# Tokens 256 to 511 first in the input projection of a decoder block

## The chip, the core and the metric

The program runs on one core of a Trainium2 chip. Its engines are TensorE (PE in the profile, with its weight loads shown apart as PEld), VectorE (DVE), ScalarE (ACT), GpSimd (POOL) and SyncE (SP, which issues the DMAs here). The metric is the device time of one execution in microseconds, as the median of several runs. All arithmetic is in 32-bit floats, and a product is formed from operands that are split into a high and a low part.

## The reference

The reference is one layer of a hybrid decoder: 16 meta tokens are put ahead of 1024 tokens of width 1024, each token is normalized, and a wide projection feeds three mixers (windowed attention with sinks and a relative bias, forgetting attention, and a gated linear recurrence). Their outputs are gated, summed and projected; a SwiGLU block and a last normalization follow. What the change touches is the beginning:

```python
h = jnp.concatenate([meta, x], axis=1)             # 16 + 1024 tokens
u = rms_norm(h, norm_mix[l])
proj = u @ w_in[l]
qa, ka, va, qf, kf, vf, fl, xc, yc, gates = jnp.split(proj, split_points, axis=-1)
```

and the table of relative biases, `rel_table[t5_bucket(dist)]`, which windowed attention adds to its scores much later.

## The kernel before

Tokens are taken in nine tiles: tile 0 holds the 16 meta tokens, tiles 1 to 8 hold 128 tokens each. A tile goes through three steps. `load_x` issues its DMA (512 KB for a full tile). `normed` (line 292) squares it on ScalarE with a sum along the row (line 297), takes the root (line 298), inverts it on VectorE (line 299) and multiplies the tile, in two halves, by that factor and the gains `gbc` (line 301). `to_feature_major` (line 198) transposes eight blocks of 128 by 128 on TensorE (line 204) into two PSUM banks, and `split` (line 115) writes the high part from each bank with ScalarE (line 118) and the low part with VectorE (line 119), into the token columns of `uh` and `ul`.

The projection is computed feature by feature. One block of 128 features needs the weights of that block, 512 KB, loaded by `load_w` and split into a high and a low tile; with `lo_on_pool=True` the low one is formed on GpSimd (line 138), otherwise on VectorE. `proj_chunk` multiplies one such block with a chunk of token columns: 8 blocks of the inner dimension, with three matmuls each (high by high, high by low, low by high; line 150), so 24 matmuls in one PSUM bank, which a sink then copies out on ScalarE. `FULL` cuts the 1040 token columns into chunks of 272, 256 and 512; `REAL` cuts the 1024 real tokens into two of 512. The columns 272 to 527 are tiles 3 and 4.

This first stage projects four blocks, `XC`, `XC+1` (inputs of the recurrence) and `YC`, `YC+1` (its gates), and forms the table of biases: a small matmul `pb` (line 321), an addition (line 322), a store to `bts` in DRAM, a load of 1.5 MB back into all partitions as `bb`, and a store of that as `bss`. Before the change the order written is: tiles 0, 1 and 2; the small loads and `pb`; the weights of `XC`; tiles 3 and 4; chunk 272 and chunk 256 of both `XC` blocks; the weights of `YC`; the other tiles among the remaining chunks.

A planner orders each engine's instructions at compile time. It takes the written order as priority, but lets an instruction go ahead of earlier ones when by its own estimate its inputs are there sooner. Engines then run their queues strictly in that order. `keep_in_program_order(i)` holds `i` behind the instruction written just before it on its engine. `issue_after(i)` holds all that a block writes for the engine of `i` behind `i`, without waiting for its end. Pools give tiles a number of buffers (4 for `xt`, the raw tokens; 2 for `wr`, the raw weights; 2 PSUM banks for transposes): a DMA into a buffer waits until the last reader of the tile before is done, and all DMAs are issued from one queue, SP's, in its order. The pool `r0` of this stage is closed after it, and the tiles of the next stages lie on the same addresses; a tile waits for the readers of those tiles that lay there.

After this stage come the blocks `XC+2` and `YC+2`, and then `values`, which loads four pieces of `w_v`, splits them into `vh` and `vl` and uses them as moving operands.

## Time and profile before

| | |
|---|---|
| median of 3 runs | 1662.85 us (1662.39 to 1664.62) |
| the profiled execution | 1662.29 us, of which the profile's span is 1660.5 us |
| TensorE matmuls busy | 1630.2 us, 98% of the span |
| VectorE, ScalarE, GpSimd busy | 999.4 us, 760.7 us, 433.1 us |
| mean granted clock of TensorE | 0.996 |

The span is cut into 40 slices of 41.5 us on the profile's page. There TensorE is at 9 tenths or more in all slices but three: the first (7), one near 1060 us (8) and the last (8). The profile's chain of work that ended last is 87% TensorE. All times of the rows below count from the start of the span.

### The profile page before, as it was taken

To read this page: it belongs to the slowest core of one execution; us is meant where nothing else is said; L and a number is where in the kernel's file an instruction comes from. 1 tells how busy PE (TensorE), PEld (TensorE's weight loads), DVE (VectorE), ACT (ScalarE), POOL (GpSimd) and SP (SyncE) were. 2 spreads that over 40 slices of the span, in tenths; PEclk is the share of its full clock that TensorE was granted. 3 is DMA by queue.
4 is the path that set the end of the run, shared out by engine and by line. 5 is a ranking of instruction groups with operands and counts; after the bars stand their busy time and mean duration, and the time that the engine had idled before them with its cause. 6 is when DMAs were issued, how large, how long until landed. Compare 5 with 4: busy or idle time off the path is not lost.

```text
span 1660.5 us, 22597 instructions
## 1 busy us (share of the span) xinstructions
PE 1630.2 (98%) x8159; PEld 1375.1 (83%) x8159; DVE 999.4 (60%) x1799; ACT 760.7 (46%) x1397; POOL 433.1 (26%) x341
## 2 busy tenths in 40 slices
PE   7999999999999999999999999899999999999998
PEld 6898978888888888888887888688888888888886
DVE  6565556555566666641348437977666676567544
ACT  6456466555555555542336434333333333345342
POOL 2111001001122221110225001776666566300000
PEclk9999999999999999999999999899999999999999
DMA  7132352223324142339737221464444443598642
GB/s 255 63 108 93 122 153 79 88 89 121 108 76 129 59 122 79 107 114 320 244 127 235 102 77 70 158 222 169 165 147 146 146 161 131 197 356 278 195 128 101
DMA packets 110879, 242.47 MB, mean 146 GB/s; under 512 B 11944, under 2 KB 23544, under 8 KB 110512
## 3 DMA queue, kind: packets, MB, share of 16 engines
q1 hardware_dynamic: 110768, 241.04, 42.7%
q8 instruction: 64, 1.05, 0.3%
q14 instruction: 47, 0.39, 0.1%
HBM read 163.45 MB, written 72.21 MB: 142 GB/s over the span
## 4 chain that ended last, share of the span: by engine, by line
PE 87%; DVE 4%; issue 4%; ACT 2%; POOL 1%; DMA 1%; SPq 0%; DVEq 0%; POOLq 0%; ACTq 0%
PE mm_w L150 26%; PE mm_s L150 13%; PE tr_s L150 7%; PE mm_br L150 6%; PE mm_wo L150 5%; PE mm_x L1086 4%; PE tr_y L1086 4%; PE sc_y L1086 4%; PE ob L547 3%; PE sc_s L150 3%; PE tr L558 3%; PE mm_v L150 2%; PE ob_x L1086 1%; PE mm_g L150 1%; PE mm_u L150 1%
## 5 line engine op out<-in xcount | busy, mean ns | idle before, releaser
L150 PE MATMUL mm_w<-uh,wh 128*128 128x512 f32 (+2 forms) x744 | 292.6, 393 | 0.0
L150 PE MATMUL mm_w<-uh,wl 128*128 128x512 f32 (+2 forms) x744 | 280.5, 377 | 0.0
L150 PE MATMUL mm_w<-ul,wh 128*128 128x512 f32 (+2 forms) x744 | 279.9, 376 | 0.0
L150 PEld LDWEIGHTS mm_w<-uh,wl 128*128 128x128 f32 x744 | 140.0, 188 | 25.7
L150 PEld LDWEIGHTS mm_w<-uh,wh 128*128 128x128 f32 x744 | 140.4, 189 | 12.7
L150 PEld LDWEIGHTS mm_w<-ul,wh 128*128 128x128 f32 x744 | 140.7, 189 | 11.7
L119 DVE TENSOR_TENSOR ab<-raw,ab 128x1024 fp32r<-128x1024 f32 x77 | 93.0, 1224 | 71.6 <-ACT ab L118 69.6
L118 ACT ACTIVATE ab<-raw 128x1024 fp32r<-128x1024 f32 x77 | 80.9, 1059 | 94.7 <-PE ob_x L1086 23.4
L150 PE MATMUL mm_s<-pt,ar 128*128 128x512 f32 x480 | 117.4, 394 | 3.7 <-ACT c L952 3.7
L118 ACT ACTIVATE wh<-wr 128x1024 fp32r<-128x1024 f32 (+1 forms) x85 | 72.7, 856 | 103.2 <-PE mm_w L150 50.6
L150 PE MATMUL mm_br<-o,wh 128*128 128x512 f32 x384 | 118.3, 389 | 0.0
L119 DVE TENSOR_TENSOR pl<-tr,ph 128x384 fp32r<-128x384 f32 (+2 forms) x160 | 87.4, 555 | 47.0 <-ACT ph L118 43.1
L150 PEld LDWEIGHTS mm_s<-pt,ar 128*128 128x128 f32 x480 | 91.5, 191 | 23.6 <-ACT c L952 4.5
L118 ACT ACTIVATE ph<-tr 128x384 fp32r<-128x384 f32 (+2 forms) x160 | 76.8, 485 | 53.6 <-PE tr L558 51.5
L119 DVE TENSOR_TENSOR wl<-wr,wh 128x1024 fp32r<-128x1024 f32 x45 | 55.6, 1235 | 72.2 <-ACT wh L118 71.9
L648 POOL TENSOR_SCALAR s<-s,sm 128x144 f32<-128x144 f32 (+3 forms) x64 | 48.6, 761 | 172.1 <-DVE sm L647 144.2
L150 PEld LDWEIGHTS mm_br<-o,wh 128*128 128x128 f32 x384 | 72.1, 188 | 14.9
L558 PE MATMUL tr<-ident,s 128*128 128x128 f32 x480 | 79.6, 274 | 1.2 <-POOL s L596 0.6
L150 PE MATMUL mm_wo<-woh,hl 128*128 128x512 f32 x256 | 79.1, 390 | 0.0
L150 PE MATMUL mm_br<-o,wl 128*128 128x512 f32 x192 | 75.3, 392 | 1.5 <-DVE wl L119 1.4
L558 PEld LDWEIGHTS tr<-ident,s 128*128 128x128 f32 x480 | 59.1, 140 | 18.3 <-DVE pl L119 3.4
L1086 PE MATMUL mm_x<-ab 128*128 128x512 f32 x297 | 72.7, 389 | 0.0
(252 smaller groups left out, 3687.9 us busy)
## 6 DMA issues: line engine op xcount, KB each, us to landing
wr<-w_in_dram SPq DMA_DIRECT2D x45, 512.0 KB, 3.7
wr<-w_fi_dram SPq DMA_DIRECT2D x44, 512.0 KB, 3.8
raw<-asp SPq DMA_DIRECT2D x77, 256.0 KB, 3.2
asp<-a SPq DMA_DIRECT2D x66, 256.0 KB, 2.5
gz<-z SPq DMA_DIRECT2D x48, 256.0 KB, 2.1
o<-osp SPq DMA_DIRECT2D x24, 512.0 KB, 6.1
sg<-gz SPq DMA_DIRECT2D x48, 256.0 KB, 3.2
fo<-w_fo_dram SPq DMA_DIRECT2D x22, 512.0 KB, 5.1
```

Source lines behind the costliest of these rows:

```text
L118: act.activation(hi, src, AF.Copy)
L119: i = dve.tensor_tensor(lo, src, f32(hi), ALU.subtract)
L150: pe.matmul(ps, a, b, start=first and i == 0, stop=i == n - 1, skip_group_check=not first)
L547: pe.matmul(ob[:, q0:q0 + b - a], vt[:, c], x[:, a:b], start=count == 0, stop=count == n_mm - 1, skip_group_check=True)
L558: pe.transpose(tb[:, col:col + P], src, ident)
L648: pool.tensor_scalar(s[:, :nk], s[:, :nk], den, 1.0, ALU.mult, ALU.mult)
L1086: pe.matmul(banks[x], a[:, 0, q], b[:, 1], start=first and j == 0 and c == 0, stop=j == NJ - 1 and c % 3 == 2, skip_group_check=True)
```

## The change

The stage is written in a new order:

- `split` returns its two instructions, and `to_feature_major` returns those of its second half.
- 16 transposes of the identity are put at the head of TensorE's work; their results are not used. After the transposes of tile 3, and again after those of tile 4, come 8 more whose results are not used.
- Tiles 3 and 4 are loaded first, the gains between them, then the weights of the two `XC` blocks. The split of each block of weights is held on ScalarE behind the second high part of tile 3 or 4, and its low part is formed on VectorE. The weights of `YC` are split on VectorE too.
- The chunk of 256 columns of both `XC` blocks is projected first; tiles 1, 2 and 0, in this order, are loaded after the weights of `XC`, and their work on ScalarE is held behind the second high part of tile 4.
- The 512 columns of `YC` that were one chunk are two of 256: columns 272 to 527 come second, columns 16 to 271 after the chunk of 272 of both `XC` blocks.
- `pb`, its addition and `nsink` are held behind all the chunks, and so the transfers `bts`, `bb` and `bss` come after them as well.

```diff
     def split(hi, lo, src, scale=None, pin=False):
 
         if scale is None:
-            act.activation(hi, src, AF.Copy)
+            a = act.activation(hi, src, AF.Copy)
             i = dve.tensor_tensor(lo, src, f32(hi), ALU.subtract)
...
+        return a.ins, i.ins
...
-            split(uh[:, ks, off:off + n], ul[:, ks, off:off + n], src)
+            last = split(uh[:, ks, off:off + n], ul[:, ks, off:off + n], src)
+        return last
...
-        xts = [load_x(t) for t in range(2)]
+        def busy(x, n, k):
+
+            for i in range(k):
+                pe.transpose(spare[:, :n], x[:n, i * P:(i + 1) * P], ident[:n, :n])
+
+        spare = o_bank("_spare")
+        for _ in range(16):
+            busy(ident, P, 1)
+
+        xts = {3: load_x(3)}
         dma(gbc, gains[0:1].partition_broadcast(P))
-        xts.append(load_x(2))
-        n0, n1 = normed(0, xts[0]), normed(1, xts[1])
-        to_feature_major(*n1)
-        n2 = normed(2, xts[2])
-        to_feature_major(*n0)
-        to_feature_major(*n2)
+        xts[4] = load_x(4)
+        raws = []
+        for m in range(2):
+            raws.append(wp.tile([P, D], F32, tag="wr", name=nm("wr")))
+            dma(raws[m], w_in[XC + m])
+        sinks = [x_sinks(ra, m) for m in range(2)]
+        wx = []
+        ns = [normed(t, xts[t]) for t in (3, 4)]
+        for n, raw in zip(ns, raws):
+
+            seen = to_feature_major(*n)[0]
+            with tc.issue_after(seen):
+                hi, lo = (r0.tile([P, D], F32R, name=nm("wx")) for _ in range(2))
+                split(hi, lo, raw)
+                wx.append((hi, lo))
+            busy(n[0], P, 8)
+        xts = {t: load_x(t) for t in (1, 2, 0)}
+        wy = [load_w(w_in[YC + m], D) for m in range(2)]
+        for m in range(2):
+            run(proj_chunk(XC + m, wx[m], FULL[1], sinks[m][0]))
+        with tc.issue_after(seen):
+            for t in (1, 2, 0):
+                norm_in(t, xts[t])
+        for m in range(2):
+            run(proj_chunk(YC + m, wy[m], (0, 272, 256, 256), sinks[m][1]))
+        for m in range(2):
+            run(proj_chunk(XC + m, wx[m], FULL[0], sinks[m][0]))
+        for t in range(5, 9):
+            norm_in(t, load_x(t))
+        for m in range(2):
+            run(proj_chunk(YC + m, wy[m], (0, NM, 256, 0), sinks[m][1]))
+        dma(part, par)
+        dma(rowt, rows.partition_broadcast(P))
 
         dma(cmt, cmask)
         rt = r0.tile([32, 8], F32, name="rt")
...
         dma(mr, maskrow.partition_broadcast(8))
+        for m in range(2):
+            run(proj_chunk(XC + m, wx[m], FULL[2], sinks[m][0]))
+        for m in range(2):
+            run(proj_chunk(YC + m, wy[m], REAL[1], sinks[m][1]))
         pb = sc_bank()
-        pe.matmul(pb[:8, :383], rt, oh, start=True, stop=True)
-        dve.tensor_tensor(mr, pb[:8, :383], mr, ALU.add)
-        sinks = [x_sinks(ra, m) for m in range(2)]
-        wx = [load_w(w_in[XC + m], D, r0, f"x{m}", lo_on_pool=True) for m in range(2)]
...
-        wy = [load_w(w_in[YC + m], D, lo_on_pool=True) for m in range(2)]
...
+        tc.keep_in_program_order(pe.matmul(pb[:8, :383], rt, oh, start=True, stop=True))
+        tc.keep_in_program_order(dve.tensor_tensor(mr, pb[:8, :383], mr, ALU.add))
+        tc.keep_in_program_order(dve.tensor_scalar(nsink, rowt[:, 0:8], -1.0, None, ALU.mult))
         dma(bts, mr)
         pad(r0, 32)
         bb = r0.tile([P, 8, 383], F32, name="bb")
         dma(bb, bts.partition_broadcast(P))
         dma(bss, bb)
...
```

## Rows read from the trace of the kernel before

**Rows 1.** Busy time of each engine in stretches of the span: the stretch and its length, then busy microseconds with the number of instructions for PE, PEld, DVE, ACT and POOL, the granted clock column, the DMA engines' share and GB/s.

```profile
0.00:9.07 9.07, 0.00 (x1) 0.03 (x1) 2.58 (x7) 4.81 (x9) 0.83 (x10) 1.00 0.74 254
9.07:15.39 6.32, 6.22 (x27) 4.20 (x27) 4.12 (x10) 5.05 (x10) 2.72 (x2) 1.00 1.00 401
15.39:19.60 4.21, 4.21 (x18) 3.98 (x18) 3.30 (x7) 3.94 (x8) 1.98 (x1) 1.00 0.67 222
31.00:68.14 37.14, 36.60 (x178) 30.31 (x177) 19.33 (x34) 14.24 (x24) 1.80 (x3) 1.00 0.33 123
100.00:1651.00 1551.00, 1537.22 (x7651) 1294.49 (x7650) 944.92 (x1702) 700.10 (x1299) 414.86 (x322) 1.00 0.43 146
```

**Rows 2.** The first DMA issues on SP's queue, in order of time: start and length of the issue (not of the transfer), then destination and source.

```profile
0.74 0.86 SPq L58 DMA_DIRECT2D xt<-h_in_dram  x2
1.65 0.42 SPq L58 DMA_DIRECT2D gbc<-gains_dram  x1
...
4.47 0.83 SPq L58 DMA_DIRECT2D wr<-w_in_dram  x2
```

**Rows 3.** The instructions of ScalarE, VectorE and TensorE around the first transposes, in order of time: start, length, engine, line, operation, and in brackets the idle time before and what ended it.

```profile
4.73 1.06 ACT L297 ACTIVATE xg<-xt 128x1024 f32<-128x1024 f32 x1 [0.41 <-DMA xt<-h_in_dram]
6.86 2.73 DVE L301 SCALAR_TENSOR_TENSOR xg<-xt,sq,gbc 16x512 f32<-16x512 f32 x4 [0.45 <-DMA gbc<-gains_dram]
8.63 1.06 ACT L297 ACTIVATE xg<-xt 128x1024 f32<-128x1024 f32 x1 [2.42 <-DMA xt<-h_in_dram]
...
9.07 1.94 PE L204 MATMUL tr<-ident,xg 128*128 128x128 f32 x8 [9.07 <-DVE xg L301]
...
10.19 0.60 ACT L118 ACTIVATE uh<-tr 128x512 fp32r<-128x512 f32 x1
10.94 1.44 PE L321 MATMUL sc<-oh,rt 32*8 32x383 f32 x2
11.01 0.68 DVE L119 TENSOR_TENSOR ul<-tr,uh 128x512 fp32r<-128x512 f32 x1
11.54 1.05 ACT L137 ACTIVATE x0h<-wr 128x1024 fp32r<-128x1024 f32 x1
```

**Rows 4.** Single matmuls of the projection in order of time, columns as in rows 3: the first, two of the chunk of 272 columns some 3.5 us later, and two later still.

```profile
15.39 0.59 PE L150 MATMUL mm_w<-uh,x0h 128*128 128x272 f32 x1
...
18.77 0.43 PE L150 MATMUL mm_w<-uh,x0h 128*128 128x272 f32 x1
19.00 0.43 PE L150 MATMUL mm_w<-ul,x0h 128*128 128x272 f32 x1
...
19.77 0.29 PE L150 MATMUL mm_w<-uh,x0l 128*128 128x272 f32 x1
19.89 0.28 PE L150 MATMUL mm_w<-uh,x0h 128*128 128x272 f32 x1
```

**Rows 5.** The same for the chunk of 256 columns, the transposes of one tile, and the last matmul of the stage, of 512 columns, with the first one of the next.

```profile
27.05 0.28 PE L150 MATMUL mm_w<-uh,x0l 128*128 128x256 f32 x1
27.17 0.28 PE L150 MATMUL mm_w<-uh,x0h 128*128 128x256 f32 x1
...
31.01 1.03 PE L204 MATMUL tr<-ident,xg 128*128 128x128 f32 x8
...
67.91 0.39 PE L150 MATMUL mm_w<-uh,wl 128*128 128x512 f32 x1
68.14 0.29 PE L150 MATMUL mm_w<-uh,wh 128*128 128x272 f32 x1
```

**Rows 6.** Low parts of weights on GpSimd and on VectorE, and a VectorE multiplication that runs beside one on GpSimd, columns as in rows 3.

```profile
28.07 2.86 POOL L138 TENSOR_TENSOR wl<-wr,wh 128x1024 fp32r<-128x1024 f32 x1
28.59 2.88 DVE L301 SCALAR_TENSOR_TENSOR xg<-xt,sq,gbc 128x512 f32<-128x512 f32 x1
...
31.58 1.42 DVE L301 SCALAR_TENSOR_TENSOR xg<-xt,sq,gbc 128x512 f32<-128x512 f32 x2
...
33.72 0.66 PE L204 MATMUL tr<-ident,xg 128*128 128x128 f32 x4 [0.54 <-DVE ul L119]
...
59.04 1.23 DVE L119 TENSOR_TENSOR bdl<-wr,bdh 128x1024 fp32r<-128x1024 f32 x1 [3.74 <-ACT bdh L118]
```

**Rows 7.** The granted clock around a long wait of TensorE later on, columns as in rows 1.

```profile
1062.90:1066.70 3.80, 0.05 (x2) 0.02 (x1) 1.99 (x2) 1.18 (x3) 3.80 (x3) 0.50 0.72 276
1066.70:1070.90 4.20, 4.20 (x10) 3.33 (x11) 4.20 (x4) 0.97 (x2) 3.49 (x4) 0.50 0.32 125
1070.90:1075.00 4.10, 4.10 (x19) 3.39 (x19) 3.96 (x4) 2.24 (x5) 3.06 (x3) 1.00 1.00 333
```

**Rows 8.** The two large transfers of the bias table on SP's queue; the time to landing of the last one, from the DMA issues of the first 62 us, and that of the weights of one block, from the page's DMA issues (count, KB of one, median microseconds); the last two low parts of `w_v`, and the first matmul that uses them.

```profile
31.33 0.42 SPq L58 DMA_DIRECT2D bb<-bts  x1
38.78 0.33 SPq L58 DMA_DIRECT2D bss<-bb  x1
...
bss<-bb SPq DMA_DIRECT2D x1, 1532.0 KB, 5.1
...
wr<-w_in_dram SPq DMA_DIRECT2D x45, 512.0 KB, 3.7
...
81.93 1.59 DVE L119 TENSOR_TENSOR vl<-wr,vh 128x656 fp32r<-128x656 f32 x2
...
92.19 0.31 PE L150 MATMUL mm_v<-vh,uh 128*128 128x328 f32 x1
```

More of the change, by code (lines that the diff above doesn't have):

```diff
@@ L122, in split @@
         else:
-            act.activation(hi, src, AF.Copy, scale=scale)
-            dve.scalar_tensor_tensor(lo, src, scale, f32(hi), ALU.mult, ALU.subtract)
+            a = act.activation(hi, src, AF.Copy, scale=scale)
+            i = dve.scalar_tensor_tensor(lo, src, scale, f32(hi), ALU.mult, ALU.subtract)
+        return a.ins, i.ins
     def load_w(src, n, pl=None, tag="w", bufs=None, lo_on_pool=False):
@@ L319, in hybrid_block @@
         dma(mr, maskrow.partition_broadcast(8))
+        for m in range(2):
+            run(proj_chunk(XC + m, wx[m], FULL[2], sinks[m][0]))
+        for m in range(2):
+            run(proj_chunk(YC + m, wy[m], REAL[1], sinks[m][1]))
         pb = sc_bank()
-        pe.matmul(pb[:8, :383], rt, oh, start=True, stop=True)
-        dve.tensor_tensor(mr, pb[:8, :383], mr, ALU.add)
-        sinks = [x_sinks(ra, m) for m in range(2)]
-        wx = [load_w(w_in[XC + m], D, r0, f"x{m}", lo_on_pool=True) for m in range(2)]
-        xs34 = [load_x(t) for t in (3, 4)]
-        n34 = [normed(t, xs34[t - 3]) for t in (3, 4)]
-        for m in range(2):
-            run(proj_chunk(XC + m, wx[m], FULL[0], sinks[m][0]))
-            if m == 0:
-                to_feature_major(*n34[0])
-                to_feature_major(*n34[1])
-        for m in range(2):
-            run(proj_chunk(XC + m, wx[m], FULL[1], sinks[m][0]))
-        xs56 = [load_x(t) for t in (5, 6)]
-        wy = [load_w(w_in[YC + m], D, lo_on_pool=True) for m in range(2)]
-        for t in range(5, 7):
-            norm_in(t, xs56[t - 5])
-        run(proj_chunk(YC, wy[0], REAL[0], sinks[0][1]))
-        for t in range(7, 9):
-            norm_in(t, load_x(t))
-        dma(part, par)
-        dma(rowt, rows.partition_broadcast(P))
-        dve.tensor_scalar(nsink, rowt[:, 0:8], -1.0, None, ALU.mult)
+        tc.keep_in_program_order(pe.matmul(pb[:8, :383], rt, oh, start=True, stop=True))
+        tc.keep_in_program_order(dve.tensor_tensor(mr, pb[:8, :383], mr, ALU.add))
+        tc.keep_in_program_order(dve.tensor_scalar(nsink, rowt[:, 0:8], -1.0, None, ALU.mult))
         dma(bts, mr)
@@ L348, in hybrid_block @@
         dma(bss, bb)
-        run(proj_chunk(YC + 1, wy[1], REAL[0], sinks[1][1]))
-        for m in range(2):
-            run(proj_chunk(XC + m, wx[m], FULL[2], sinks[m][0]))
-        for m in range(2):
-            run(proj_chunk(YC + m, wy[m], REAL[1], sinks[m][1]))
     r1 = ctx1.enter_context(tc.tile_pool(name="r1", bufs=1, side="right", reuse_waits="tile"))
```

## The prediction

> **What bounds the kernel now.** I read busy time by stretches first, because the page gives TensorE 98% of the span and the change touches the first 70 us alone. From 100 us on TensorE is busy 1537.2 of 1551 us [rows 1]. What is moved at the beginning therefore reaches the end of the program one for one: a microsecond by which the next stage starts earlier is a microsecond of the result, as long as nothing later waits instead. The stage ends where the first matmul of the next one starts, at 68.14 us [rows 5]; that is the mark against which I sum.
>
> Within it TensorE does nothing for 9.07 us [rows 1]. Read in order of time, what it waits for is a chain: the first full tile has landed by 4.73, the gains by 6.86, VectorE does three multiplications of about 0.68 us (2.73 for four), and the first transposes start at 9.07 [rows 3]. The first matmul of the projection follows at 15.39 [rows 4]. In the 6.3 us between, TensorE shows as busy, yet does only three tiles' transposes and `pb`. From 15.39 to 68.14 there are 52.75 us, nearly without a gap: 0.54 us of waiting in the stretch from 31 on [rows 1, 6].
>
> The second loss is the clock. The clock column reads 1.00 from the start [rows 1], but the matmuls don't bear that out: those of 272 columns start 0.23 us apart at 18.8, which is 272 columns at 1.2 GHz, and 0.12 apart at 19.8, which is 2.4 GHz [rows 4]. The 18 matmuls between 15.39 and 19.6 [rows 1] ran at the lower level, though TensorE had worked on transposes since 9.07 [rows 3]. Near 1067 us the same is seen with the column at 0.50: after a wait of 3.8 us, TensorE is busy without a gap for 4.2 us before the full clock is back [rows 7]. So both times it took about 4.2 us of projection-like matmuls.
>
> **The change, part by part.** The sum is made against the profiled execution, 1662.29 us, of which 1660.5 are span and 1.8 lie outside it, where nothing changes. The median of the runs is 0.56 higher; I add the difference to the median, 1662.85.
>
> *Start of the projection.* Tile 3 is alone ahead of the gains, in place of a small and a full tile. Its own landing comes a little sooner, but it needs the gains, which stay second in the queue [rows 2]: between 6.4 and 6.9. One multiplication of 0.68 us follows instead of three, so its transposes start near 7.4 instead of 9.07. Eight at the lower clock take 1.94 us [rows 3], the eight extra ones as long: 11.3. Tile 4 lands as the third load, at or before 8.63; the third load of before was squared at 8.63 and through its first multiplication when the low part at 11.01 followed on VectorE [rows 3], so the extra transposes delay nothing yet. Tile 4's transposes take until 13.2, the extra ones behind them until 15.1.
>
> The other two engines: ScalarE does the high parts of tile 3 (two of 0.60) from 10.2, the first weights (1.05) until 12.4, the high parts of tile 4 until about 13.7, then the second weights [rows 3]. VectorE has from 10.3 two multiplications (0.7 each), four low parts of tokens (0.68) and the first weights' low part, now 1.23 on VectorE against 2.9 on GpSimd [rows 6]: 5.4 us if packed, and the projection can start when the first low part of tile 4 is there, one part before the end: 15.0, or 13.8 if that goes ahead of the weights' low part. The weights are issued before the other tiles now, fourth and fifth; they land before ScalarE gets to them. So the start lies between 13.8 and 15.1; I take 14.6: **-0.8 us**. The extra transposes cost up to 1.3 of it if the planner leaves them where they are written, nothing if it does not.
>
> *Work that moves behind the start.* In both orders 48 full transposes lie behind it (tiles 3 to 8 before; 1, 2 and 5 to 8 now). New behind it are the eight narrow transposes of tile 0 (at most 8 x 0.13 by a full tile's 1.03 for eight [rows 5], at least almost nothing; I take 0.5), and `pb`, which stood where TensorE had nothing else to do and took 1.44 at the lower clock [rows 3]: 0.7 at the full one. Two chunks of 512 columns become four of 256: 48 times 0.23 against 48 times twice 0.12 [rows 5], so 0.01 x 48 = 0.5 (0 to 1 by the rounding). Together **+1.7 us** (0.7 to 2.7).
>
> *Clock.* If it again needs 4.2 us of projection, the loss is half of 4.2, 2.1, instead of 18 x 0.103 = 1.85: **+0.2 us**. If the transposes bring it up first, -1.85: that is the first rival. The trace of before has no stretch of transposes alone that is long enough to decide it, so both stand as bounds.
>
> *GpSimd leaves.* A multiplication took 2.88 us beside GpSimd's `wl`, 0.7 alone [rows 6]; the wait of 0.54 us for a low part stands behind that crowd. It goes: **-0.5 us**. VectorE gets 4 x 1.23 = 4.9 us more work, but was busy only 19.3 of 37.1 us from 31 on [rows 1]; the cover is the 11 us and more of projection that the two `XC` chunks and the two new `YC` chunks give before tiles 1, 2 and 0 are wanted. Were it gone, a late tile would cost about 1 us each. The weights of `YC` wait for the raw buffers of `XC`, freed by the low parts at about 14.5 and 17; with 3.7 us to land [rows 8] and 2.3 for the splits they are there by 21 and 23, when TensorE has just done the two `XC` chunks (14.6 + 2 x 2.9, and 2 for the clock: 22.4). Next to late is thus the second one; I take 0.
>
> *The bias table.* `bts`, `bb`, `bss` go behind the whole stage; SP's queue is held while `bb` waits for `bts` and `bss` for `bb`, with the loads of `w_v` behind them. Cost 0 if it fits, else the third rival.
>
> Sum: -0.8 + 1.7 + 0.2 - 0.5 = **+0.6 us**, 1662.85 + 0.6 = **1663.5 us**. The start is gained, and spent on work that used to lie in front of it for nothing.
>
> The Trainium skill, "TensorE: Matmul & The Clock Gate", section "Part 4: PE-mode transpose", holds that transposes do not bring TensorE to its full clock, as they don't count as work in the way matmuls do. This speaks against the 16 and 2 x 8 extra transposes: by it the time is the 1663.5 above, without it the first rival's. Rows 3 and 4 agree with it as far as they go (about 2 us of transposes at 9.07, and the lower clock at 15.39), but would look the same if the stretch was only too short.
>
> **The rivals.**
>
> *1. The transposes raise the clock* before the projection starts. For it: they keep TensorE busy from about 7.4 on, longer than the 4.2 us of rows 7. Against it: the lower clock after those of before [rows 3, 4]. The tile transposes then take 1.03 instead of 1.94, VectorE sets the start, 14.2: -1.2 + 1.7 - 1.85 - 0.5 = -1.85, **1661.0 us**.
>
> *2. The chains pack better than I wrote*: the low parts of tokens go ahead of those of the weights, and the weights land as fast as 400 GB/s allows [rows 1]: about 10, plus 1.05 and 1.23, so the projection starts at 12.2, with the clock up: -3.2 + 1.7 - 1.85 - 0.5 = -3.85, **1659.0 us**. Against it: tile 4 is multiplied only at 11.1, and every later step is a queue of parts on two engines.
>
> *3. The late bias table stalls the next stage* (the slower side). By the sizes in the code `bb` starts 51 KB into `r0`, where after 38 KB of `r1` the tiles of `values` lie, so `vl` waits until `bss` has read `bb`. Before, that was over at 38.78 + 5.1 = 43.9 [rows 8]. Now `pb` and its addition end at about 69.5; `bts`, 12 KB, takes between nothing and the 5.1 of `bss`, I take 2; `bb` 7.45 (31.33 to 38.78), `bss` 5.1 [rows 8]: 84.1. Two pieces of `w_v` can wait in their buffers; the other two are loaded after the first low parts, so 0.8 + 3.7 + 0.8 + 0.8 later, at 90.2 to 91. Before, the last low part ended at 83.5, and TensorE uses the first at 92.19 [rows 8], the last pieces 18 matmuls of 0.14 (328 columns at 2.4 GHz) later, near 95. So 4 us are left. It decides when the loads of `w_v` lie behind `bb` on the DMA rings: up to 7.45 us later, that is 3.5 to 4 of waiting: **1667.3 us**.
>
> *That the change does not do what it says*, the planner scattering the extra transposes among the projection: at most 32 x 0.13 = 4 us, most likely under 1; I count it with the forecast.
>
> **How the numbers follow.** A measurement of this kernel tells a change from none at about 0.2%, 3.3 us: below 1659.5 is faster, above 1666.2 slower. Chances: forecast 0.46, rival 1 0.26, rival 2 0.12, rival 3 0.16. Faster holds most of rival 2 and the lower edge of rival 1, 0.16; slower most of rival 3 and little of the forecast, 0.16; within, 0.68. The forecast with its bounds (start 13.8 to 15.1, moved work 0.7 to 2.7) is 1661.7 to 1665.0; the range reaches to rival 2 and most of the way into rival 3: 1658.8 to 1667.0.
>
> **What would show it.** Right if the first matmul on `x` weights starts at 14 to 15, if matmuls of 256 columns start 0.21 apart for about 4 us there and 0.12 after, if `YC`'s chunks wait for nothing, and if the next stage's first matmul starts at 68 to 69.5. The clock step is wrong if the first matmuls of the projection already start 0.12 apart. The start is wrong if it is below 13.5. Waits of TensorE on `vl` or `vh` at 90 to 100 would show rival 3. Tiles 1 and 2 making TensorE wait between 22 and 32 would show that the cover on VectorE was too thin.

## The result, and the profile after

The changed kernel has a median of 1664.98 us (1663.13 to 1666.49, 18 runs); the kernel before, run beside it on the same chips, 1662.40 us (1660.70 to 1664.62, 18 runs). The ratio is 1.0016, 95% interval 1.0009 to 1.0022: 2.6 us slower, less than the 0.2% that was set as the bound. The forecast was 1663.5 us, its range 1658.8 to 1667.0.

The profiled execution of the changed kernel took 1665.63 us, its span 1663.8 us; TensorE's matmuls were busy 1635.9 us of it (98%), VectorE 1002.5, ScalarE 755.7, GpSimd 426.1, and the mean granted clock was 0.995. Marks that both traces have, in microseconds from the start of the span, show where the difference arises (`vst` holds the parts into which the results of `values` are split, `s` the scores of windowed attention, `c` a tile of the last stages):

| mark | before | after | after minus before |
|---|---|---|---|
| first matmul of the projection | 15.39 | 13.75 | -1.64 |
| first matmul of the next stage | 68.14 | 67.70 | -0.44 |
| matmul behind the 1.1 us wait for `vst` | 169.26 | 171.53 | +2.27 |
| first transposes of the scores `s` | 252.70 | 256.19 | +3.49 |
| matmul behind the wait for `c` | 1066.68 | 1070.38 | +3.70 |
| end of the span | 1660.5 | 1663.8 | +3.3 |

The stage that was rewritten ends earlier. The loss lies between 68 and 256 us, where the change put nothing but the transfers of the bias table. From 100 to 1651 us TensorE is busy 1537.13 us, as before [rows 1].

TensorE's instructions at the head, in the order of time (start, length, engine, line, operation, count, and in brackets the idle time before and what ended it):

```profile
1.45 3.67 PE L309 MATMUL ob_spare<-ident 128*128 128x128 f32 x16 [1.45 <-POOL ident masks.py:199]
7.51 1.23 PE L205 MATMUL tr<-ident,xg 128*128 128x128 f32 x8 [2.39 <-DVE xg L303]
8.57 1.04 PE L309 MATMUL ob_spare<-ident,xg 128*128 128x128 f32 x8
10.39 0.30 PE L309 MATMUL ob_spare<-ident,xg 128*128 128x128 f32 x1 [0.78 <-DVE xg L303]
11.56 0.66 PE L205 MATMUL tr<-ident,xg 128*128 128x128 f32 x4 [0.87 <-DVE ul L119]
...
12.66 1.44 PE L309 MATMUL ob_spare<-ident,xg 128*128 128x128 f32 x6
13.75 0.56 PE L151 MATMUL mm_w<-uh,wx 128*128 128x256 f32 x1
14.11 0.41 PE L151 MATMUL mm_w<-ul,wx 128*128 128x256 f32 x1
...
16.43 0.28 PE L151 MATMUL mm_w<-ul,wx 128*128 128x256 f32 x1
```

The first eight transposes take 1.23 us and the eight idle ones behind them 1.04; before, eight took 1.94 [rows 3] and, later and at the full clock, 1.03 [rows 5]. So the 16 idle ones had raised the clock. The six idle ones that start at 12.66 take until 13.75, 0.18 each, and the first matmuls start 0.21 apart: it had fallen again. The view by stretches says the same (stretch, length, busy time with count for PE, PEld, DVE, ACT and POOL, granted clock, DMA share, GB/s):

```profile
7.51:12.75 5.24, 3.59 (x27) 2.94 (x28) 3.94 (x7) 3.85 (x7) 0.00 (x0) 0.99 1.00 378
12.75:13.75 1.00, 1.00 (x7) 1.00 (x6) 1.00 (x2) 1.00 (x3) 0.00 (x0) 0.50 0.95 270
13.75:16.20 2.45, 2.45 (x14) 2.45 (x13) 1.91 (x3) 2.45 (x4) 0.00 (x0) 0.52 0.91 242
16.20:67.70 51.50, 51.50 (x337) 45.86 (x335) 21.96 (x38) 22.29 (x48) 0.09 (x1) 1.00 0.24 78
```

Between 13.75 and 67.70 TensorE waits for nothing. Behind the stage it does. These are lines of VectorE, GpSimd and TensorE from there, columns as at the head:

```profile
67.81 0.55 DVE L364 TENSOR_TENSOR mr<-sc,mr 8x383 f32<-8x383 f32 x1 [4.08 <-PE sc L363]
...
69.56 0.80 DVE L384 TENSOR_SCALAR x<-xr,part 128x1040 f32<-128x1040 f32 x1
...
91.61 0.84 DVE L119 TENSOR_TENSOR vl<-wr,vh 128x656 fp32r<-128x656 f32 x1
...
93.61 2.37 POOL L394 TENSOR_TENSOR th<-th,y 128x1024 f32<-128x1024 f32 x1
...
93.65 3.03 DVE L119 TENSOR_TENSOR vl<-wr,vh 128x656 fp32r<-128x656 f32 x1
...
96.73 0.42 PE L151 MATMUL mm_v<-vl,uh 128*128 128x328 f32 x1 [1.79 <-DVE vl L119]
```

VectorE stands for 4.08 us in front of `mr`, the addition of the bias table, which is held at the end of the stage. Behind it in the queue is the work of the recurrence: `x` starts at 69.56, though ScalarE had written the `xr` that it reads by 51.16. Before, the same operation stood at 53.14:

```profile
53.14 0.82 DVE L367 TENSOR_SCALAR x<-xr,part 128x1040 f32<-128x1040 f32 x1 [9.28 <-ACT xr L269]
```

Part of that work are the weights of the gates, `bd`. Their split is later still: ScalarE has queued the high part `bdh` behind drains of the next stage (a drain is the copy of a finished PSUM bank), VectorE stands idle for it, and the low part `bdl` comes at 80.90, not at 59.04 [rows 6]. Until `bdl` is done, the raw weights keep their buffer, and SP's queue, which had stood 6.0 us for `bb` to land, stands another 5.2 us for `bdl` before it can issue the other three pieces of `w_v`. After, then the issues of `w_v` before:

```profile
50.56 0.60 ACT L271 ACTIVATE xr<-mm_w 128x512 f32<-128x512 f32 x1 [5.21 <-PE mm_w L151]
...
79.81 1.05 ACT L118 ACTIVATE bdh<-wr 128x1024 fp32r<-128x1024 f32 x1
...
80.90 1.23 DVE L119 TENSOR_TENSOR bdl<-wr,bdh 128x1024 fp32r<-128x1024 f32 x1 [9.19 <-ACT bdh L118]
...
82.15 10.66 SPq L58 DMA_DIRECT2D wr<-w_v_dram  x3
```

```profile
65.07 12.70 SPq L58 DMA_DIRECT2D wr<-w_v_dram  x4
```

So that work, 16 to 22 us later, meets the low parts of `w_v`, which are later for its sake and were over by 83.5 before [rows 8]. The third of them takes 3.03 us instead of 0.84 beside a GpSimd multiplication from 93.61 to 95.98 (`th`, part of the gates), and TensorE waits 1.79 us for it. After this wait the clock is at half for 3.4 us, which costs half of it, 1.7 us:

```profile
98.00:101.40 3.40, 3.40 (x14) 3.22 (x13) 2.91 (x10) 1.81 (x3) 0.00 (x0) 0.50 0.36 140
101.40:110.00 8.60, 8.60 (x58) 8.47 (x57) 3.03 (x7) 8.06 (x11) 2.44 (x1) 1.00 0.30 106
```

The waits of TensorE between 60 and 260 us that bear on it (engine, line and what it waited for: total, times, longest). First after, then before:

```profile
PE mm_v L151 <- DVE vl L119: 1.8, 1, 1.8
...
PE mm_v L151 <- DVE vst L119: 1.5, 2, 1.1
```

```profile
PE mm_v L150 <- DVE vst L119: 1.4, 2, 1.1
...
PE mm_v L150 <- DVE zall L468: 1.2, 1, 1.2
```

The wait for `vl` stands in place of a wait of 1.21 us for `zall`, so it costs 0.6 more; with 1.7 for the clock that is 2.3 of the 2.7 us lost between the marks at 68 and 170. The next 1.2 us hold a wait of 0.99 us for `sm`, VectorE's pass over the scores, behind loads of the biases that took longer to land (`nb`, 5.1 us from issue to landing, 2.8 before).

The 1.7 us for the clock belong to the profiled execution. The mean granted clock of every timed execution is on record, and 3.4 us at half lower it by 0.001. It is 0.997 in 87 of the 101 executions of the kernel before that ran beside the experiments, and in 8 of the 18 of the changed kernel; these 8 take 1664.1 us in the mean, the other ten, at 0.993 to 0.996, 1665.3. So recorded falls of the clock, at the head or behind a wait, make 1.2 us of difference between the two groups, and without them the changed kernel is still 1.7 us above the kernel before.

### The profile page after: what moved, and what is told of

The parts are those of the page before. It is cut to its first block, busy times and chain, and to the rows that moved or that the text cites. A ratio compares the mean times of both kernels' runs of the same rounds, so it can differ in the third digit from the quotient of the medians.

```text
span 1663.8 us, 22764 instructions
## 1 busy us (share of the span) xinstructions
PE 1635.9 (98%) x8239; PEld 1382.1 (83%) x8239; DVE 1002.5 (60%) x1803; ACT 755.7 (45%) x1395; POOL 426.1 (26%) x337
## 3 DMA queue, kind: packets, MB, share of 16 engines
q8 instruction: 65, 1.06, 0.3%
```

## The experiments

Twelve kernels ran. The ratio is to the kernel before, run beside them on the same chip. The theories, by the letters of the expectations: A, `pb` and its addition at the end cost the time; B, the late transfers `bts`, `bb`, `bss` do; C, the new head pays nothing by itself; D, added after the first runs, the order in which ScalarE and VectorE do the recurrence's side work (its drains, the small log-sigmoid chain `ls`, the gates) sets what TensorE waits for later.

**The bias chain late in the old kernel.** The kernel before, with the chain behind the stage's last matmuls, as the change has it:

```diff
-        pb = sc_bank()
-        pe.matmul(pb[:8, :383], rt, oh, start=True, stop=True)
-        dve.tensor_tensor(mr, pb[:8, :383], mr, ALU.add)
...
             run(proj_chunk(YC + m, wy[m], REAL[1], sinks[m][1]))
+        pb = sc_bank()
+        tc.keep_in_program_order(pe.matmul(pb[:8, :383], rt, oh, start=True, stop=True))
+        tc.keep_in_program_order(dve.tensor_tensor(mr, pb[:8, :383], mr, ALU.add))
+        tc.keep_in_program_order(dve.tensor_scalar(nsink, rowt[:, 0:8], -1.0, None, ALU.mult))
+        dma(bts, mr)
...
```

> The kernel before with only the bias table's chain (with its three places held) moved behind the stage, all else as it was. Theories A and B: the same loss as in the changed kernel without its gain in the head, 2.5 to 4 us over the kernel before: 1665 to 1666.5, with a wait on vl near 97 and the clock down there. Theory C: no change, 1662 to 1663.

1665.53 us, ratio 1.0020 [1.0011, 1.0029]. The old head with this one part of the change costs as much as the whole change. The stage ends at 69.39 (+1.25: `pb`, 0.73, now lies on the path, and waits within the stage are 1.09 instead of 0.54), and the wait on `vl` is there to the hundredth:

```profile
95.29 2.37 POOL L377 TENSOR_TENSOR th<-th,y 128x1024 f32<-128x1024 f32 x1
...
95.33 3.03 DVE L119 TENSOR_TENSOR vl<-wr,vh 128x656 fp32r<-128x656 f32 x1
...
98.41 0.42 PE L150 MATMUL mm_v<-vl,uh 128*128 128x328 f32 x1 [1.79 <-DVE vl L119]
```

With the stage's 1.25, this wait's 0.6 net of the one for `zall`, 0.8 for `cum` near 155 and 0.4 for `sm` near 247, two waits that the kernel before does not have, the 2.9 us between the two spans are complete; what made these two is not shown. In this profiled execution no fall of the clock follows, and 6 of the 11 timed ones have a mean clock of 0.997 and take 1665.5 as well: here the clock is not what costs. In this run the first of the recurrence's operations, `ls`, also stands 0.9 us until the store `bts` has read `mr`, though it uses neither; it seems to lie where `mr` lay, so here the memory holds it too. In the changed kernel it is not memory that holds `x` back: the next run, with the same tiles, has it at 52.60.

**The chain ahead of the last two loops.** The changed kernel, with:

```diff
-        for m in range(2):
-            run(proj_chunk(XC + m, wx[m], FULL[2], sinks[m][0]))
-        for m in range(2):
-            run(proj_chunk(YC + m, wy[m], REAL[1], sinks[m][1]))
         pb = sc_bank()
...
         dma(bss, bb)
+        for m in range(2):
+            run(proj_chunk(XC + m, wx[m], FULL[2], sinks[m][0]))
+        for m in range(2):
+            run(proj_chunk(YC + m, wy[m], REAL[1], sinks[m][1]))
```

> The changed kernel with the whole chain of the bias table (pb, its addition to mr, nsink, bts, bb, bss) written ahead of the last two loops of the stage (XC of the third part, YC of the second). Theory A (pb's late place pushes the whole side work of the recurrence back beside values): the side work returns to about 45 to 60 us, TensorE no longer waits for vl near 97, the clock stays up there, the first gate matmul goes back to about 79; that is the 3 us of the loss and some of the head's gain: 1661 to 1662.5 us. Theory B (the late transfers of the table cost, by SP's queue and the buffers' memory): the same time, since the transfers are early too. Theory C (the head itself, with the work moved behind the start, costs): still 1664 to 1665.5.

1665.43 us, 1.0021 [1.0012, 1.0029]: a miss for A and B, and in the range of C. The wait on `vl` is gone and the time stays, because another takes its place, twice as long as the one of before at this spot. `zall` is the last reading of a bank of `values` by VectorE, which frees it for the next matmuls.

```profile
117.88 0.39 PE L151 MATMUL mm_v<-vh,uh 128*128 128x328 f32 x1 [2.50 <-DVE zall L485]
```

The stretch behind it, by the view of busy time, where 0.50 is the granted clock:

```profile
119.30:122.70 3.40, 3.40 (x15) 3.40 (x14) 3.40 (x7) 0.44 (x1) 0.00 (x0) 0.50 0.96 385
```

The stage ends at 68.18, as before, so the trace puts the loss behind it. Upstream of `zall` lie the gates, and ScalarE does them later: the step `r` starts at 87.41 (84.11 before), `q` at 90.93 (89.29). The first thing that is late on ScalarE is the table load of `ls`, at 63.55 behind a drain that waits for TensorE, against 59.03 before; `ls` itself starts on VectorE at 51.66, not 43.71:

```profile
62.94 0.60 ACT L274 ACTIVATE y<-mm_w 128x512 f32<-128x512 f32 x1 [3.89 <-PE mm_w L151]
63.55 1.28 ACT L163 ACT_TABLE_LOAD   x1
```

**Only `pb` and its addition early,** the transfers left at the end of the text. The changed kernel, with:

```diff
         dma(mr, maskrow.partition_broadcast(8))
+        pb = sc_bank()
+        tc.keep_in_program_order(pe.matmul(pb[:8, :383], rt, oh, start=True, stop=True))
+        tc.keep_in_program_order(dve.tensor_tensor(mr, pb[:8, :383], mr, ALU.add))
         for m in range(2):
             run(proj_chunk(XC + m, wx[m], FULL[2], sinks[m][0]))
...
-        pb = sc_bank()
-        tc.keep_in_program_order(pe.matmul(pb[:8, :383], rt, oh, start=True, stop=True))
-        tc.keep_in_program_order(dve.tensor_tensor(mr, pb[:8, :383], mr, ALU.add))
```

> The changed kernel with only pb and its addition to mr ahead of the last two loops; bts, bb and bss stay late, behind them. Theory A: side work of the recurrence at 45 to 60 again, no wait on vl, 1661 to 1662.5 us. Theory B: w_v's loads still lie behind bb, so TensorE waits for vl 1.5 to 4 us near 97 and the time stays at 1664 to 1666. Theory C: 1664 to 1665.5 as well, but without a wait on vl.

1665.22 us, 1.0017 [1.0008, 1.0026]. No wait on `vl`, as C expected; 2.42 us for `zall` at 117.17, as in the run before, here without a fall of the clock. This profiled execution is among the quickest: two of the eleven have a mean clock of 0.996 or 0.997 and take 1663.5 and 1663.8, the nine at 0.994 and 0.995 take 1665.5 in the mean. Moving `pb` and its addition is enough to take the wait on `vl` away. What the run can't show is late transfers alone. Their place in the text is late, but SP's queue has nothing ahead of them once the addition is done, and issues them at 46 to 54 us:

```profile
46.11 0.30 SPq L58 DMA_DIRECT2D bts<-mr  x1
47.49 0.33 SPq L58 DMA_DIRECT2D bb<-bts  x1
53.60 0.32 SPq L58 DMA_DIRECT2D bss<-bb  x1
```

**Without the idle transposes.** The changed kernel, with:

```diff
-        spare = o_bank("_spare")
-        for _ in range(16):
-            busy(ident, P, 1)
...
-            busy(n[0], P, 8)
```

> The changed kernel without its 32 extra transposes (16 on ident, 8 after each of the two tiles). If they raised the clock and that brought the start forward: tile 3's eight transposes take about 1.9 instead of 1.23, the projection starts at 14.3 to 14.8 instead of 13.75, and the clock rises 2.5 to 4 us after that start, as in the kernel before; together 0.5 to 1.2 us longer, 1665.5 to 1666.2. If they bring nothing: the start at 13.2 to 13.8, 0 to 0.5 us shorter, 1664.5 to 1665.

1665.06 us, 1.0016 [1.0007, 1.0025]: the same as the changed kernel. The clock differs as it should if the transposes raise it: a tile's eight take 1.94 us again, the matmuls run at half until 17.8, and the stage ends 0.85 us later, at 68.55 instead of 67.70. The start is a miss: it was expected at 14.3 to 14.8 and came at 13.35, 0.40 earlier than with the idle transposes. The 0.85 is not seen in the median. The wait on `vl` is 1.8 us here too, and in this execution no fall of the clock follows it. The recorded clocks say why the two may come out alike: none of the 11 timed executions here is below 0.996, and 7 of the 18 of the changed kernel are, so the idle transposes go with more recorded falls (the low clock at the head here stands under a column of 1.00 and isn't counted).

```profile
7.49 1.94 PE L205 MATMUL tr<-ident,xg 128*128 128x128 f32 x8 [7.49 <-DVE xg L303]
...
13.35 0.58 PE L151 MATMUL mm_w<-uh,wx 128*128 128x256 f32 x1
...
68.55 0.39 PE L151 MATMUL mm_w<-uh,wh 128*128 128x272 f32 x1
```

**The chain early and the log-sigmoid in the projection too.** The edit of the second run, and:

```diff
         dma(rowt, rows.partition_broadcast(P))
+        log_sigmoid(lsc[:, 1], part[:, P_LM:P_LM + 4], r0, [P, 4])
+        dve.tensor_scalar(lsc[:, 0], lsc[:, 1], -4.0, None, ALU.mult)
+        dve.tensor_scalar(lsc[:, 1], lsc[:, 1], 8.0, None, ALU.mult)
...
-        log_sigmoid(lsc[:, 1], part[:, P_LM:P_LM + 4], r1, [P, 4])
```

> The changed kernel with the table's chain ahead of the last two loops, and the small log-sigmoid of the recurrence's decay (ls, lsc: 25 operations on VectorE of 0.15 us, one table load on ScalarE) also done there instead of in the next stage. Theory D (what costs is the order of the recurrence's side work on ScalarE and VectorE in the next stage: whatever is late there ends in the wait of TensorE for vl or for zall, and in a clock that falls in it): the table load no longer stands behind the drain of y, the gates' drains end 1 to 2 us earlier than in the run with the chain early, the wait for zall at 117 falls from 2.5 to 1.2 or less, the clock stays up there: 1661.5 to 1663 us. Theory C (the head's extra work itself costs): the wait gets shorter and the time stays at 1664.5 to 1665.5.

1664.69 us, 1.0011 [1.0003, 1.0020]. The wait for `zall` is back to what it was before the change:

```profile
116.80 0.39 PE L151 MATMUL mm_v<-vh,uh 128*128 128x328 f32 x1 [1.22 <-DVE zall L485]
```

So it was the place of `ls` that had doubled it, which speaks for D. The time does not: D expected 1661.5 to 1663, and a shorter wait with 1664.5 to 1665.5 is what C expected. The profiled execution lost elsewhere: a wait of 1.76 us for `sm` at 246.65, and half clock from 247.8 to 251.2.

**The same move in the old kernel**, the control for D. The kernel before, with the same three lines moved to the same place:

```diff
         dma(rowt, rows.partition_broadcast(P))
+        log_sigmoid(lsc[:, 1], part[:, P_LM:P_LM + 4], r0, [P, 4])
...
-        log_sigmoid(lsc[:, 1], part[:, P_LM:P_LM + 4], r1, [P, 4])
```

> The kernel before with that log-sigmoid moved into the projection stage, nothing else. Theory D: the side work there was in time but for 1.2 us of waiting for zall, so the gain is at most these 1.2 us: 1661.3 to 1662.6. Theory C says nothing of it; if the 25 operations hold up the tokens' chain on VectorE, 1663 to 1664.

1666.91 us, 1.0030 [1.0019, 1.0042], the slowest of all and above every range that was expected. The 25 small operations now stand on VectorE among the low parts of the tokens, and TensorE waits for one, with half clock from 36.1 to 39.5:

```profile
35.95 0.79 PE L204 MATMUL tr<-ident,xg 128*128 128x128 f32 x3 [2.79 <-DVE ul L119]
```

The wait for `zall` is 1.23, no shorter than in the kernel before. Moving `ls` pays only where its old place was late.

**Idle transposes in the old kernel.** The kernel before, with:

```diff
+        spare = o_bank("_spare")
+        for _ in range(36):
+            busy(ident, P, 1)
+
         xts = [load_x(t) for t in range(2)]
```

> The kernel before with 36 idle transposes of the identity at the start, nothing else: the part of the change that should raise the clock, alone. If they raise it: the tokens' transposes at about 9 take 1.2 instead of 1.9 us, the first projection matmuls of 272 columns start 0.12 apart instead of 0.24, the stage ends 2.5 to 3.5 us earlier, and since the recurrence's side work hangs on that stage it comes earlier too: 1659.5 to 1661.5 us. Rival: the clock stays low until projection matmuls have run, as without them; then 36 transposes at 0.23 are 8.3 us, end at 9.7 and push the first tile back by 0.6: 1662.5 to 1663.5. Second rival: the clock rises but the gain is lost in the wait for zall, which grows by as much: 1662 to 1662.8.

1664.49 us, 1.0011 [1.0003, 1.0020], above all three ranges. The clock came up and was lost again:

```profile
9.06 1.23 PE L204 MATMUL tr<-ident,xg 128*128 128x128 f32 x8 [2.10 <-DVE xg L301]
...
13.90 2.26 PE L204 MATMUL tr<-ident,xg 16*128 16x16 f32 x12 [2.87 <-DVE ul L119]
...
17.52 0.58 PE L150 MATMUL mm_w<-uh,x0h 128*128 128x272 f32 x1
```

The 2.87 us come from ScalarE. With more work of TensorE ahead, the planner had put the high parts of both blocks of weights, 1.06 each at 10.21 and 11.48, in front of the high parts `uh` of the tokens at 12.45. The projection starts 2.1 us later than before, the stage ends at 69.53.

**More idle transposes.** The kernel of the fifth run, with:

```diff
-        for _ in range(16):
+        for _ in range(30):
...
             busy(n[0], P, 8)
+            if len(wx) == 1:
+                for _ in range(2):
+                    busy(n[0], P, 8)
```

> The run with the chain and the log-sigmoid early, and TensorE kept busy ahead of the projection: 30 idle transposes instead of 16, and 24 instead of 8 behind the first tile, so that no wait of 0.8 us or more is left between 1.5 and 13. If the waits of 2.4, 0.8 and 0.9 us are what lets the clock fall (or keeps it from rising) ahead of the projection: the first projection matmuls start 0.12 apart in every execution, 0.5 to 1.5 us less than the run without them: 1660.5 to 1662. If not: the same time within 0.5 us.

1666.20 us, 1.0023 [1.0013, 1.0032], above both ranges. The same kind of loss, by another operation: the Exp of `ls`, which waits 3.31 us for VectorE (there the first step of `ls` waits for the load of `part`), went ahead of `uh` on ScalarE, and the stage ends at 72.77.

```profile
15.73 0.20 ACT L163 ACTIVATE ls<-ls 128x4 f32<-128x4 f32 x1 [3.31 <-DVE ls L162]
...
16.47 0.58 PE L151 MATMUL mm_w<-uh,wx 128*128 128x256 f32 x1 [2.84 <-ACT uh L118]
```

**The old order with idle transposes and the queues held by hand.** The kernel of the seventh run with 28 idle transposes at the head and 8 behind each of tiles 1 and 2, VectorE's and ScalarE's work held behind the parts of the tokens. The core of it:

```diff
+        s1 = to_feature_major(*n1)
+        busy(n1[0], P, 8)
+        n2 = normed(2, xts[2], s1[0][1])
+        s0 = to_feature_major(*n0)
+        s2 = to_feature_major(*n2)
+        busy(n2[0], P, 8)
...
+        for m, seen in enumerate((s1[1][0], s0[1][0])):
+            with tc.issue_after(seen):
+                wx.append(load_w(w_in[XC + m], D, r0, f"x{m}", lo_on_pool=True))
```

> The kernel before with idle transposes (28 on the identity, 8 on each of the first two wide tiles) and, as in the change, a forced order where the planner would otherwise put work that looks ready ahead: tile 1 normalized before tile 0, the casts of the XC weights behind the first two tiles' high parts on ScalarE, the bias table's addition behind tile 1's low parts and tiles 3 and 4 behind tile 2's on VectorE. Theory K (idle transposes raise the clock, and the run with 36 of them alone lost it again only because ScalarE cast the weights ahead of the tokens, so that TensorE waited 2.9 us): first projection matmul at 13.5 to 14.5 instead of 15.39, its 272-column matmuls 0.12 apart from the first on, stage end 2.5 to 4 us earlier, 1659 to 1661 us. Rival: the 2 to 4 us come back as waits in the next stage (zall, vl) or in the last: 1662 to 1664. Second rival: a wait of 0.7 us or more remains ahead of the start and the clock falls there, as in the changed kernel: start at 14, slow matmuls for 3 to 7 us, 1661 to 1662.5.

1666.18 us, 1.0023 [1.0014, 1.0032]. A miss: the order came out as written, the start at 17.53, 2.14 later than before. A multiplication of 0.7 us on VectorE took 2.79, until 15.14, beside GpSimd's low part of the weights:

```profile
12.25 2.35 POOL L139 TENSOR_TENSOR x0l<-wr,x0h 128x1024 fp32r<-128x1024 f32 x1 [10.86 <-ACT x0h L138]
...
12.35 2.79 DVE L306 SCALAR_TENSOR_TENSOR xg<-xt,sq,gbc 128x512 f32<-128x512 f32 x1
```

**The log-sigmoid where VectorE is idle**, right behind `nsink`, held there. The kernel of the fifth run, with:

```diff
-        tc.keep_in_program_order(dve.tensor_scalar(nsink, rowt[:, 0:8], -1.0, None, ALU.mult))
+        neg = tc.keep_in_program_order(dve.tensor_scalar(nsink, rowt[:, 0:8], -1.0, None, ALU.mult))
+        with tc.issue_after(neg.ins):
+            log_sigmoid(lsc[:, 1], part[:, P_LM:P_LM + 4], r0, [P, 4])
...
```

> The changed kernel with the table's chain ahead of the last two loops and the log-sigmoid right behind it on VectorE, where that engine sat idle at 46 to 51 (in the run before last it stood at 16, between the tokens). Theory D (the order of the side work is what cost): wait for zall 1.2 or less, no wait for vl, no clock fall there, start of the projection at 13.3 to 14 as in the changed kernel: 1662.5 to 1664, better than the changed kernel by 1 to 2 us. Rival (what is left over the kernel before is the head's own work: YC's first 512 columns in two parts, the narrow tile behind the start, the table's matmul): no better than 1663.5 whatever the side work does, since the stage ends at 67.5 to 68.2 at best.

1663.83 us, 1.0008 [0.9999, 1.0017]. No wait on `vl`, 1.22 for `zall` at 116.33, no fall of the clock there; the stage ends at 68.21, no earlier than before. This is the first version whose interval holds no change. The time lies in the range of D and in that of its rival, by which the head's own work is what is left.

**`pb` ahead of the projection as well**, where it stood before the change. The kernel of the tenth run, with:

```diff
+        dma(rt, relt)
+        dma(oh, onehot)
+        dma(mr, maskrow.partition_broadcast(8))
         sinks = [x_sinks(ra, m) for m in range(2)]
...
+            if len(wx) == 1:
+                pb = sc_bank()
+                pe.matmul(pb[:8, :383], rt, oh, start=True, stop=True)
...
+        with tc.issue_after(low):
+            dve.tensor_tensor(mr, pb[:8, :383], mr, ALU.add)
```

> The run with chain and log-sigmoid in the idle stretch, and the bias table's matmul with its three small loads moved ahead of the projection, between the first tile's idle transposes and the second tile, where TensorE waited 0.7 us; its addition stands behind the second tile's low parts on VectorE. If what is left over the kernel before is work of TensorE behind the start: the 0.73 us of that matmul leave the stage, which ends 0.7 us earlier, and the time falls by as much, 1662.5 to 1663.5 us. Rival (the next stage's side work sets the time, not the stage's end): no change, 1663.5 to 1664.3, with the wait for zall 0.5 us longer or more. Rival 2 (the three loads and the addition stand in the way of tokens and weights): start 0.5 to 1 us later, 1664 to 1665.

1663.27 us, 1.0005 [0.9996, 1.0014], the lowest of the changed ones. `pb` took 1.44 us at half clock in front of the projection, as before [rows 3], which started at 15.69; the stage ends at 68.56. The time is in the range expected, but not for the reason given: the stage was to end 0.7 us earlier than in the tenth run and ends 0.35 later. The 0.56 us between the two medians therefore has no cause shown, and the intervals overlap.

**The same without the idle transposes.** The kernel of the eleventh run, with:

```diff
-        spare = o_bank("_spare")
-        for _ in range(16):
-            busy(ident, P, 1)
...
-            busy(n[0], P, 8)
```

> The run with the table's matmul ahead of the projection, without the 32 extra transposes; the order on VectorE and ScalarE in the next stage is the same. If the transposes pay (the clock is up for the tokens' transposes and for part of the first projection matmuls): the stage ends 0.8 us later or more and the time is 0.5 to 1.2 us longer than with them. If their gain is lost again in the wait ahead of the second tile, where the clock falls: within 0.4 us.

1664.24 us, 1.0013 [1.0004, 1.0021]. The stage ends at 69.48, 0.92 later than with them, and the median is 0.97 higher. With no wait on `vl` and the wait for `zall` at its old length, what the transposes gain at its end is seen in the time; the two intervals overlap, so the size rests on the marks as much as on the medians.

No version beats the kernel before, so none is recommended in its place.

**What the runs decide.** A late bias chain alone costs the old kernel 3 us (first run), with the same wait on `vl`; taken back, the wait goes (second and third run), so that wait is the chain's. In every run the transfers moved in time with `pb` and its addition; that the queue behind the addition makes the wait, and not the transfers, is read from the traces. A and B as explanations of the whole loss fall, since the time stays. D is supported by three traces, in which the wait for `zall` goes from 2.4 or 2.5 to 1.2 with the place of `ls`, and by ratios of 1.0011, 1.0008 and 1.0005 against 1.0021 in the second run, though all of these intervals overlap. C stands in part: the stage ends 0.4 us earlier in the changed kernel, 0.5 in the third run, and no earlier than before in the second, fifth, tenth and eleventh. Each of these marks is from one execution, and with the same head the projection starts at 13.75 (changed kernel), 14.11 (second run) and 13.26 (third run), so 0.5 us between single marks says little.

## Why the prediction was right and wrong

The time, 1664.98, is 1.5 us above the forecast and in the range; the class, within 0.2%, was the one given 0.68. By steps it is right only in sum.

*Start of the projection:* forecast 14.6, measured 13.75, below the lower bound of 13.8 that was given to VectorE's queue. The tile's transposes started at 7.51, as forecast (7.4). They took 1.06 until the next instruction, not 1.94, and the idle ones behind them 1.04: the clock of the transposes was wrong. Yet the clock is not what made the start early, since the fourth run, with its transposes at 1.94, starts at 13.35. The step that failed is VectorE's queue: its multiplications for tile 4 were put at 10.3, where those of the third load had stood before, and came at 9.49.

```profile
9.49 1.42 DVE L303 SCALAR_TENSOR_TENSOR xg<-xt,sq,gbc 128x512 f32<-128x512 f32 x2
```

In the changed kernel the projection starts where the last idle transposes end, at 13.75; by these two executions they cost 0.40 at the start.

*Work moved behind the start:* forecast +1.7, measured +2.65. The narrow transposes took 0.70 (0.5 forecast) and `pb` 0.73 (0.7). The mis-sized term is the cut of `YC`'s chunks: 0.5 was forecast; 96 matmuls of 512 columns had taken 22.6 us without their wait, and 96 of 256 with 48 of 512 took 12.81 + 11.00 = 23.8, so 1.2. The rounding of 0.23 and 0.12 to two digits was the bound of 1 for this, and it was too tight.

*Clock:* forecast +0.2, measured -1.1. Of the first 48 matmuls those of before lost 2.3 us (8.36 in place of 48 times 0.126), those of after 1.2. The sign named for it, 0.21 apart and then 0.12, was seen, yet for 2.45 us and not for 4; it could not tell a clock that never rose from one that rose and fell, which is what happened. Rival 1 had the mechanism and not the size, since it had no fall in it.

The forecast drew on the Trainium skill, "TensorE: Matmul & The Clock Gate", section "Part 4: PE-mode transpose", by which transposes do not bring the full clock. For the 32-bit transposes of this kernel the trace disagrees: after 16 of them in 3.67 us the next eight took 1.23 us and not 1.94, and the measurement decides.

*GpSimd leaves:* -0.5 forecast, the 0.54 us gone. *Cover for tiles 1, 2 and 0:* as forecast, no wait from 13.75 to 67.70.

Start and the rest of the stage together: forecast +0.6, measured -1.64 + 2.65 - 1.1 - 0.54 = -0.6 from the terms and -0.44 by the mark. The forecast of the stage's end, 68 to 69.5, was missed at 67.70.

*The bias table at nothing* is the step that failed outright. It was costed by its transfers alone; late in the old kernel it costs 3.0 us by the medians (first run), of which 1.25 are in the stage itself. The wait on `vl` comes by way of VectorE's queue: the addition waits for `pb`, `pb` for the end of the stage, and behind the addition stood the recurrence's work, 16 us late, with `bdl` and the buffer of `w_v` behind it. The prediction named nothing that was queued behind that addition. Why the planner also put `bdh` behind the next stage's drains on ScalarE, no run shows. Rival 3 had the place right, a wait on `vl` at 90 to 100, and its size was 3.5 to 4 us; measured were 1.79, and 0.6 net of the wait for `zall` that it replaced, with 1.7 for the clock. Its mechanism, `vl` held by memory under `bb` and loads behind it on the rings, is not what set the wait. The loads of `w_v` were late, as it had it, but the last that they waited for was `bdl`, 5.2 us after `bb` had landed. `vh` for the third piece was formed at 92.28 and its low part could start at 93.65; alone it would have been done 0.84 later, at 94.5, and TensorE wanted it at 94.94. What made it too late was 2.3 us of standing beside GpSimd. Late transfers with an early addition were not made, so what they would cost by themselves stays open.

That the sum came near is chance: a stage 1.0 us better than forecast, and 3.0 us behind it (2.6 by the medians and the 0.44) that were priced at nothing. Falls of the clock behind the same wait were in some executions and not in others; 10 of the 18 have a lower mean clock than the 0.997 usual before, but in how many the fall is behind this wait stays open, and it was not tried to take GpSimd's `th` multiplication away from `vl`.

## What to carry to other kernels

When an operation is moved to the end of a stage and held there, list what its engine has queued behind it, and which buffers that work sets free: the price is the lateness of that work, not the operation's own 0.55 us, and it shows up where the work meets other loads, 30 us on. A gain in front of a saturated engine counts only after a look at the next waits, since removing one here twice uncovered another of 2.4 to 2.5 us; and idle instructions shift the order that a planner chooses on the other engines, which cost more than the clock gave in the seventh and eighth run.

## What was not expected of the hardware

*The clock and transposes.* With nothing but transposes TensorE came to the level of 2.4 GHz: eight took 1.23 us after 16 idle ones and after 36 (changed kernel and seventh run), 1.94 without (fourth run). It fell again behind idle times of 0.78 and 0.87 us in the changed kernel, and around one of 2.87 in the seventh run. Later on, 1.79 us of waiting were followed by half clock in the changed kernel and not in the first and fourth run; 2.50 were in the second run, 2.42 were not in the third. So a wait of about 2 us cost its own length in some executions and 1.7 us more in others. The clock column reads 1.00 until its first change: before, matmuls at 0.23 us stand under 1.00 [rows 1, 4].

*VectorE beside GpSimd.* An operation with two tensor inputs in SBUF was not done until a GpSimd multiplication that had started before it had ended: 3.03 us for 0.84 (`vl`: 2.33 until GpSimd's end at 95.98, and 0.70), 2.79 for 0.7 (`xg`, ninth run: 2.25 until GpSimd's end at 14.60, and 0.54). Even one of four columns was held, `ls` with 2.35 us for 0.16. It went the other way too: the GpSimd multiplication at 84.79 began while VectorE's `x` ran until 85.80, and took 3.26 us where the next one of its kind took 2.37. In the profile such an operation looks busy, not waiting; its length, against its own kind elsewhere, gives it away:

```profile
84.79 3.26 POOL L394 TENSOR_TENSOR th<-th,y 128x1024 f32<-128x1024 f32 x1
...
85.72 2.35 DVE L166 TENSOR_TENSOR ls<-ls,ls 128x4 f32<-128x4 f32 x1
```

The Trainium skill, "SBUF — State Buffer", section "SBUF: two separate sides", gives the rule: VectorE and GpSimd share a pair of ports, and where VectorE reads two inputs from SBUF and GpSimd reads SBUF too, whichever starts first has it for the whole instruction. The trace agrees: GpSimd's start and length and the 0.84 of an undisturbed `vl`, 93.61 + 2.37 + 0.84, give 96.82, and this `vl` ended at 96.68.
